# Which queue issues the stores of turned rows and of the softmax heads' outputs: GpSimd's in place of SP's

## The chip, the cores and the metric

The kernel runs on one core of one Trainium2 chip. The metric is the device time of one execution in microseconds, as the median of several runs. The engines are called PE (TensorE, with PEld for its weight loads), DVE (VectorE), ACT (ScalarE), POOL (GpSimd) and SP (SyncE). SP computes nothing here; it issues DMA transfers.

## The reference

One layer of a decoder: 512 tokens, width 2048, FFN width 5632, everything in float32.

```python
h = rms_norm(x, norm1_g)
qa, ka, va, ra, ga, qb, kb, vb = split(h @ w_in)
out_a = gla_mixer(qa, ka, va, ra, log_sigmoid(ga @ gla_gate_w2 + gla_gate_b) / 16)  # 4 heads, chunks of 64
out_b = dilated_mixer(rms_norm(qb), rms_norm(kb), vb, rel_bias)   # 8 softmax heads of width 128, three patterns
x = x + concat([out_a, out_b]) @ w_out
h2 = rms_norm(x, norm2_g)
x = x + (silu(h2 @ w_gate) * (h2 @ w_up)) @ w_down
```

## The kernel before

**Products.** All projections run as pairs of 512-column blocks. A pair is computed as seven block products P1 to P7 in the manner of Strassen (`Pair`, `stream`), so its operands are sums and differences of quarters of the rows, and its weights sums and differences of quarters of the weight matrix. Float32 is reached by splitting: every operand tile and every weight tile is parted into a high part (a cast on ACT, L174 for operands, L331 for weights, `wh`) and a low part (a subtraction on DVE, L175 and L335, `wl`). PE multiplies high by high and low, and low by high (L372). Weights come in quarters of 512 KB on SP's queue (L222, buffers `wa` to `wd`, 12 in all), and DVE forms their sums (L256). A product of PE on a `wl` can't start before DVE has made that `wl`, and DVE works in the order of its program.

**Stages.** In order of time:

- 0 to about 525 us: the input projection, five pairs and a first one of its own form; between its matmuls, the heads of the gated linear attention and the softmax heads (`dil_head`, two at a time, lanes 0 and 1). A softmax head's output `ot` (tile oT in lane 0, r in lane 1) is stored to `mix_d[4 + h // 2]` at L1040, 8 stores.
- to about 600: the last pair of the input projection, the gate (`final_gate`). The gated rows are transposed into tiles called `turned` and stored to `mix_d`, 8 stores. Meanwhile the operands of the output projection are read back from `mix_d` (`early_jobs` and `late_jobs`, loads at L1198 into `top` and r, at L1242 into work tiles v, T, qT, kT) and split.
- 600 to 745: two pairs of the output projection. `final_out` adds the residual; `first_columns` and `scaled_store` scale the rows, transpose them and store them to `xn_d`, 16 stores. They are read back as the operands of the FFN (`opn`). In the second pair `output_scales` computes the token scales `rs2`: two small additions on DVE (L1428, L1429) and five small operations on POOL (L158, L1431, L159, L1432, L1433).
- 745 to 1560: eleven FFN pairs of gate and up columns. `final_ffn` multiplies silu of the one by the other, transposes, and stores to `p_d`, 44 stores. `sums_job` reads `p_d` back a little later, forms the sums that the last projection needs, and stores them to `S_d`.
- 1560 to the end: the down projection, six pairs.

**Turned rows.** Everything that goes to `mix_d` from the gate, to `xn_d` and to `p_d` passes `transposed_store`: PE transposes 128x128 blocks (L1134), ACT evacuates them (L1142, or L1145 with gains) into oT and PT, of which there is one buffer each, or into a spare tile `turned`; then the tile is stored (L1149), as 256 rows of 1 KB. `done` records that these rows may be read back.

**Order.** `store` and `load` are both `nc.sync.dma_start` (L146, L147), so all stores and loads stand in one queue on SP, in the order of the program, and each waits at the head of that queue for what it needs. Side work (heads, operand jobs, sums) is kept in a list `background` and in lists of deferred steps (`later`, `soon`); `p.step()` lets some of it be written into the program in the middle of each weight tile's matmuls. A scheduler then orders the instructions within each engine.

POOL has little to do: two memsets, the reciprocal roots of the norms (`rsqrt_mean`, L157 to L159) and `output_scales`. It issues no store before the change.

Of the kernel before, what the change touches and what calls it, by code (L numbers as in the profile page):

```python
# [107 lines left out]
def block_kernel(ctx: ExitStack, tc: tile.TileContext, ins, out):  # L108
    nc = tc.nc
# [18 lines left out]
    def nm(s):  # L128
        uid[0] += 1
        return f"{s}_{uid[0]}"  # L130

    def dram(shape, name):
        return dr.tile(shape, F32, name=name, tag=name)

    def bank():
        return ps.tile([P, 512], F32, name=nm("bank"), tag="bank")

    def work(tag, shape=(P, 512), bufs=1):
        return mp.tile(list(shape), F32, name=nm(tag), tag=tag, bufs=bufs)
# [7 lines left out]
    store = nc.sync.dma_start  # L147
# [237 lines left out]
    def soon(fn, groups=1):  # L385

        soonest.append([groups, fn])
# [445 lines left out]
    mix_d = [dram([P, 2, 512], f"mix_d{b}") for b in range(8)]  # L833

    def head_cols(src, h, w=P):
        return src.rearrange("(t p) c -> p t c", p=P)[:, :, h * w : (h + 1) * w]
# [117 lines left out]
    def dil_head(h, lane):  # L954


        s = h // 4

        def tile_(name):
            if lane == 0:  # L960
                return work("oT" if name == "o" else name)
            if name in "qk":
                return work(name + "T")
            return rpool.tile([P, 512], F32, name=nm("r"), tag="r")

        def logits(b):
            if lane == 0:
                return work("L", bufs=2)
            return tile_("L") if b % 2 else work("PT")

        qh, kh, vh = tile_("q"), tile_("k"), tile_("v").rearrange("p (t d) -> p t d", t=4)
        load(qh.rearrange("p (t d) -> p t d", t=4), head_cols(proj[f"qb{s}"], h % 4))
        load(kh.rearrange("p (t d) -> p t d", t=4), head_cols(proj[f"kb{s}"], h % 4))
        load(vh, head_cols(proj[f"vb{s}"], h % 4))
        tb = tile_("T")
        load(tb, bass.AP(
            tensor=rep_d.tensor, offset=h * P * NB + P - 1, ap=[[NB - 1, P], [1, 512]]
        ))
        yield
        for src, g in ((qh, gq), (kh, gk)):  # L980
            tp = bank()
            for t in range(4):
                nc.tensor.transpose(tp[:, t * P : (t + 1) * P], src[:, t * P : (t + 1) * P], ident)
            nc.scalar.activation(src, tp, AF.Copy, scale=g)
        yield
        ot = tile_("o")
        lgs = {}

        def scores(b):
            n = P * (b + 1)  # L990
            lp = bank()
            nc.tensor.matmul(lp[:, :n], qh[:, b * P : (b + 1) * P], kh[:, :n], start=True, stop=True)  # L992
            lg = lgs[b] = logits(b)
            st = work("mx", (P, 4), bufs=4)

            def rest():
                nc.vector.tensor_tensor_reduce(
                    lg[:, :n], lp[:, :n], tb[:, 512 - n :], -1.0, 3.0e38, ALU.add, ALU.min,
                    st[:, 0:1],
                )  # L1000
                nc.scalar.activation(
                    lg[:, :n], lg[:, :n], AF.Exp, scale=-1.0, bias=st[:, 0:1],
                    accum_out=st[:, 2:3],
                )

                def scaled():
                    nc.vector.reciprocal(st[:, 3:4], st[:, 2:3])
                    nc.vector.tensor_scalar(lg[:, :n], lg[:, :n], st[:, 3:4], None, op0=ALU.mult)

                soon(scaled)  # L1010

            return rest

        def turn(b, tp):
            n = P * (b + 1)
            for k in range(b + 1):
                nc.tensor.transpose(  # L1017
                    tp[:, k * P : (k + 1) * P], lgs[b][:, k * P : (k + 1) * P], ident
                )
            return lambda: nc.scalar.copy(lgs[b][:, :n], tp[:, :n])  # L1020

        def values(b, op):
            for k in range(b + 1):
                nc.tensor.matmul(  # L1024
                    op, vh[:, k, :], lgs[b][:, k * P : (k + 1) * P], start=(k == 0), stop=(k == b)
                )
            return lambda: nc.scalar.copy(ot[:, b * P : (b + 1) * P], op)

        for i in range(6):
            rests = []  # L1030
            tp = bank() if 1 <= i <= 4 else None
            if i >= 2:
                op = tp[:, i * P : (i + 1) * P] if i < 4 else bank()[:, :P]
                rests.append(values(i - 2, op))
            if tp is not None:
                rests.append(turn(i - 1, tp))
            if i < 4:
                rests.append(scores(i))
            if i == 5:
                rests.append(lambda: store(mix_d[4 + h // 2][:, h % 2, :], ot))  # L1040
            yield rests

    def dil_heads(h):
# [83 lines left out]
    def transposed_store(tiles, half, dsts, gains=None, spare=None):  # L1127

        for b in range(2):
            bk = bank().rearrange("p (j n) -> p j n", j=2)  # L1130
            for jj in range(2):
                for m in range(2):
                    f = (2 * b + jj) * P
                    nc.tensor.transpose(  # L1134
                        bk[:, jj, m * P : (m + 1) * P], tiles[m][:, f : f + P], ident
                    )
            if spare is None:
                d = work(("oT", "PT")[b], (P, 2, 256))
            else:
                d = spare[:, b]  # L1140
            if gains is None:
                nc.scalar.copy(d, bk)  # L1142
            else:
                for jj in range(2):
                    nc.scalar.activation(  # L1145
                        d[:, jj, :], bk[:, jj, :], AF.Copy,
                        scale=gains[:, 2 * b + jj : 2 * b + jj + 1],
                    )
            store(dsts[b][:, :, half * 256 : (half + 1) * 256], d)  # L1149
            done.add((id(dsts[b]), half))  # L1150

    onorm = {}
# [7 lines left out]
    def final_gate(half, which, tiles, acc_):  # L1160
        og = onorm.pop((half, which))
        if tiles is None:
            tiles = [cpool.tile([P, 512], F32, name=nm("cr"), tag="C") for _ in range(2)]
            src = acc_
        else:
            src = tiles
        for m in range(2):
            if src is acc_:
                nc.vector.scalar_tensor_tensor(
                    halves(og[m]), unfolded(src[m]), row_scale(half, m), halves(og[m]),  # L1170
                    op0=ALU.mult, op1=ALU.mult,
                )
                neg = nrs1[:, 2 * half + m : 2 * half + m + 1]
                nc.scalar.activation(halves(tiles[m]), unfolded(src[m]), AF.Exp, scale=neg)
            else:
                nc.vector.tensor_tensor(og[m], src[m], og[m], op=ALU.mult)
                nc.scalar.activation(tiles[m], src[m], AF.Exp, scale=-1.0)
            nc.scalar.activation(tiles[m], tiles[m], AF.Ln, bias=1.0)
            nc.scalar.activation(tiles[m], tiles[m], AF.Exp, scale=-1.0)

        def rest():
            for m in range(2):
                nc.vector.tensor_tensor(tiles[m], tiles[m], og[m], op=ALU.mult)
            spare = apool.tile([P, 2, 2, 256], F32, name=nm("turned"), tag="A")
            later(1 + (src is tiles), lambda: transposed_store(
                tiles, half, mix_d[2 * which : 2 * which + 2], spare=spare
            ))

        soon(rest, 2)
# [153 lines left out]
    def scaled_store(tiles, rows, half, dsts, k0, tags=None):  # L1343
        xs = []
        for m in range(2):
            s = work(tags[m]) if tags else work("L", bufs=2)
            nc.scalar.activation(s, tiles[m], AF.Copy, scale=prox[:, rows[m] : rows[m] + 1])
            xs.append(s)
        return lambda: transposed_store(xs, half, dsts, g2[:, k0 : k0 + 4])
# [284 lines left out]
```

## Time and profile before

| | us |
|---|---|
| median of 3 runs | 1964.63 (1964.08 to 1965.51) |
| profiled execution, its own time | 1963.27 |
| span of the profiled execution | 1961.5 |

The mean granted clock of PE in it is 0.998. Views of the profile used below: the line of the engines gives busy time, its share of the span, and the number of instructions. Windows give, for a stretch of time, its length and the busy time of each engine, then the granted clock, the busy share of the DMA engines and GB/s. Waits give, for an engine and a line, what it waited for: the total, how many times, and the longest. The chain of waits lists what released what, ending with the last instruction. The timeline lists single instructions: start, length, engine, line, operation, output and inputs, and in brackets the idle time before it with what ended it. For a DMA that an engine issues, the timeline's length is the issue alone; the time until the data has landed stands in the chain and in the list of DMA issues.

### The profile page before, as it was taken

What the parts mean: (1) busy time and instruction counts of PE and PEld (TensorE: products, weight loads), DVE (VectorE), ACT (ScalarE), POOL (GpSimd) and SP (SyncE); (2) the same over time, 40 slices, a digit from 0 to 9 for tenths busy, and PEclk for the clock granted to TensorE, in tenths of its full rate; (3) what the DMA queues carried; (4) which work ended last, traced back from release to release, by engine and by line L of the source; (5) the groups of instructions that cost most, each with busy time, mean ns of one, the idle gap of its engine ahead of it and who ended that gap; (6) DMA issues with size and microseconds to landing.
All of it is one profiled execution on the core that took longest, in us unless ns stands there. A gap on an engine that the chain in (4) does not pass through costs nothing.

```text
span 1961.5 us, 25794 instructions
## 1 busy us (share of the span) xinstructions
PE 1924.8 (98%) x9226; PEld 1670.7 (85%) x9226; DVE 1653.7 (84%) x1851; ACT 1094.3 (56%) x1600; POOL 61.3 (3%) x81
## 2 busy tenths in 40 slices
PE   8999999999999999999999999999999999999999
PEld 6888888888878877888888888888888888888888
DVE  8997787868789889879878878878879989989987
ACT  8564564566766766545545445445546646546443
POOL 0000230010000000000000000000000000000000
PEclk9999999999999999999999999999999999999999
DMA  8457355464666685554553554554555865955761
GB/s 279 137 164 271 107 179 165 134 208 128 215 220 205 214 294 161 173 167 134 178 169 129 177 164 128 177 162 128 177 162 162 299 207 179 317 178 176 248 214 65
DMA packets 237258, 360.45 MB, mean 184 GB/s; under 512 B 18263, under 2 KB 97056, under 8 KB 237129
## 3 DMA queue, kind: packets, MB, share of 16 engines
q1 hardware_dynamic: 236776, 358.59, 57.2%
q8 instruction: 72, 1.18, 0.2%
q14 instruction: 58, 0.47, 0.1%
q10 hardware_dynamic: 352, 0.21, 0.0%
HBM read 296.59 MB, written 64.51 MB: 184 GB/s over the span
## 4 chain that ended last, share of the span: by engine, by line
PE 82%; DVE 8%; DMA 3%; issue 3%; ACT 2%; POOL 1%; SPq 0%; DVEq 0%; ACTq 0%
PE acc L372 74%; PE acc L440 3%; DVE wl L335 3%; DVE wa L256 2%; PE bank L1134 1%; DVE AS L175 1%; PE bank L992 1%; ACT wh L331 1%; DMA xn_d<-oT 1%; PE bank L1024 1%; DMA r<-xn_d 0%; PE bank L777 0%; PE bank L1017 0%; DMA qT<-S_d 0%; DVE AA L175 0%
## 5 line engine op out<-in xcount | busy, mean ns | idle before, releaser
L372 PE MATMUL acc<-wh,AS 128*128 128x512 f32 x3008 | 711.4, 379 | 0.7 <-ACT wh L331 0.6
L372 PEld LDWEIGHTS acc<-wh,AS 128*128 128x128 f32 x3008 | 569.0, 189 | 81.8 <-ACT wh L331 1.9
L331 ACT CAST wh<-wa 128x1024 fp32r<-128x1024 f32 x376 | 394.0, 1048 | 392.3 <-PE acc L372 366.6
L372 PE MATMUL acc<-wh,AA 128*128 128x512 f32 x2256 | 534.8, 380 | 0.0
L335 DVE TENSOR_TENSOR wl<-wa,wh 128x1024 fp32r<-128x1024 f32 x376 | 456.6, 1217 | 70.3 <-ACT wh L331 45.1
L372 PEld LDWEIGHTS acc<-wh,AA 128*128 128x128 f32 x2256 | 427.3, 190 | 61.1 <-ACT wh L331 0.6
L372 PE MATMUL acc<-wl,AS 128*128 128x512 f32 x1504 | 395.4, 385 | 10.4 <-DVE wl L335 10.1
L372 PEld LDWEIGHTS acc<-wl,AS 128*128 128x128 f32 x1504 | 279.5, 189 | 62.5 <-DVE wl L335 21.8
L372 PE MATMUL acc<-wl,AA 128*128 128x512 f32 x1128 | 297.3, 386 | 6.9 <-DVE wl L335 6.7
L372 PEld LDWEIGHTS acc<-wl,AA 128*128 128x128 f32 x1128 | 209.8, 189 | 39.1 <-DVE wl L335 10.1
L331 ACT CAST wh<-wb 128x1024 fp32r<-128x1024 f32 x94 | 98.5, 1049 | 130.1 <-PE acc L372 125.1
L331 ACT CAST wh<-wc 128x1024 fp32r<-128x1024 f32 x94 | 98.4, 1047 | 112.0 <-PE acc L372 104.9
L331 ACT CAST wh<-wd 128x1024 fp32r<-128x1024 f32 x94 | 98.5, 1048 | 105.5 <-PE acc L372 102.0
L256 DVE TENSOR_TENSOR wa<-wc,wa 128x1024 f32<-128x1024 f32 x94 | 114.5, 1222 | 46.0 <-DMA wc<-in_w_gate 24.8
L335 DVE TENSOR_TENSOR wl<-wc,wh 128x1024 fp32r<-128x1024 f32 x94 | 114.7, 1220 | 36.3 <-ACT wh L331 36.1
L335 DVE TENSOR_TENSOR wl<-wd,wh 128x1024 fp32r<-128x1024 f32 x94 | 114.4, 1220 | 35.7 <-ACT wh L331 28.9
L335 DVE TENSOR_TENSOR wl<-wb,wh 128x1024 fp32r<-128x1024 f32 x94 | 113.8, 1217 | 5.7 <-ACT wh L331 5.7
L256 DVE TENSOR_TENSOR wb<-wd,wb 128x1024 f32<-128x1024 f32 x94 | 114.4, 1217 | 1.0 <-DMA wd<-in_w_in 0.5
L256 DVE TENSOR_TENSOR wa<-wb,wa 128x1024 f32<-128x1024 f32 x94 | 113.6, 1219 | 0.8
L256 DVE TENSOR_TENSOR wa<-wd,wa 128x1024 f32<-128x1024 f32 x94 | 112.8, 1216 | 0.1
L298 DVE SCALAR_TENSOR_TENSOR seed<-acc,rs,seed 128x512 f32<-128x512 f32 x96 | 70.5, 745 | 24.6 <-PE acc L372 24.5
L282 ACT ACTIVATE seed<-acc,rs 128x512 f32<-128x512 f32 x96 | 60.6, 681 | 1.4 <-PE acc L372 0.8
(306 smaller groups left out, 1366.6 us busy)
## 6 DMA issues: line engine op xcount, KB each, us to landing
wa<-in_w_gate SPq DMA_DIRECT2D x44, 512.0 KB, 3.8
wb<-in_w_up SPq DMA_DIRECT2D x44, 512.0 KB, 4.1
wd<-in_w_up SPq DMA_DIRECT2D x44, 512.0 KB, 4.3
wc<-in_w_gate SPq DMA_DIRECT2D x44, 512.0 KB, 3.6
wc<-in_w_in SPq DMA_DIRECT2D x28, 512.0 KB, 3.7
wa<-in_w_in SPq DMA_DIRECT2D x24, 512.0 KB, 5.3
wb<-in_w_in SPq DMA_DIRECT2D x24, 512.0 KB, 6.0
wd<-in_w_in SPq DMA_DIRECT2D x24, 512.0 KB, 6.7
```

What stands on the lines that cost most here:

```text
L175: nc.vector.tensor_tensor(a[:, :, 1, :], src, a[:, :, 0, :].bitcast(F32), op=ALU.subtract)
L256: nc.vector.tensor_tensor(src, self.quarter(one, g), src, op=ALU.subtract)
L282: nc.scalar.activation(halves(t), unfolded(src[m]), AF.Copy, scale=self.scale(half, m))
L298: nc.vector.scalar_tensor_tensor(halves(seed[m]), unfolded(src[m]), self.scale(half, m), halves(seed[m]), op0=ALU.mult, op1=ALU.add,)
L331: nc.scalar.copy(high[k], sources[k])
L335: nc.vector.tensor_tensor(low[k], sources.pop(k), high[k].bitcast(F32), op=ALU.subtract)
L372: nc.tensor.matmul(p.dst[prod][m], a[:, jj, hl, m * P : (m + 1) * P], folded(w[:, jj, :]), start=fresh and g == 0 and len(terms) == 2 and ...
L440: recent["pe"] = nc.tensor.matmul(dst[prod][m], a[:, jj, hl, m * P : (m + 1) * P], folded(w[:, jj, :]), start=fresh and g == 0 and len(ter ...
L992: nc.tensor.matmul(lp[:, :n], qh[:, b * P : (b + 1) * P], kh[:, :n], start=True, stop=True)
L1024: nc.tensor.matmul(op, vh[:, k, :], lgs[b][:, k * P : (k + 1) * P], start=(k == 0), stop=(k == b))
L1134: nc.tensor.transpose(bk[:, jj, m * P : (m + 1) * P], tiles[m][:, f : f + P], ident)
```

## The change

Two stores go to `nc.gpsimd.dma_start` in place of `nc.sync.dma_start`. The store in `transposed_store` moves 68 stores (8 to `mix_d` from `turned`, 16 to `xn_d`, 44 to `p_d`), the one in `dil_head` 8 more. Each is 256 KB. Sizes, addresses and what is read back stay as they are, and all loads and all other stores stay on SP.

```diff
@@ dil_head
             if i == 5:
-                rests.append(lambda: store(mix_d[4 + h // 2][:, h % 2, :], ot))
+                rests.append(lambda: nc.gpsimd.dma_start(mix_d[4 + h // 2][:, h % 2, :], ot))
@@ transposed_store
-            store(dsts[b][:, :, half * 256 : (half + 1) * 256], d)
+            nc.gpsimd.dma_start(dsts[b][:, :, half * 256 : (half + 1) * 256], d)
             done.add((id(dsts[b]), half))
```

The scheduler answers with small changes of order: on DVE and ACT around 553 to 600 us and 735 to 750 us, on SP where the loads close up around the missing stores. In POOL's program two stores of `xn_d` from the second pair stand directly behind the five operations of `output_scales`.

## The prediction

> **What bounds the kernel now.** I read the engines' line first, then the windows, then the waits of PE and of SP's queue, then the chain of waits and, at the places it pointed to, the timeline.
>
> ```profile
> PE 1924.8 (98%) x9226; PEld 1670.7 (85%) x9226; DVE 1653.7 (84%) x1851; ACT 1094.3 (56%) x1600; POOL 61.3 (3%) x81
> ```
>
> PE is busy for 1924.8 of the span's 1961.5 us. All the time that a better placed store could give back is the difference, 36.7 us. A store that comes late costs only where PE then runs dry. The windows (length, then busy time of PE, PEld, DVE, ACT and POOL, the clock, the DMA share, GB/s) say where that is:
>
> ```profile
> 500.00:560.00 60.00, 58.05 (x331) 50.54 (x331) 42.35 (x77) 41.78 (x85) 0.00 (x0) 1.00 0.79 250
> 560.00:600.00 40.00, 34.00 (x146) 27.07 (x146) 39.06 (x47) 25.47 (x38) 0.00 (x0) 0.96 0.44 147
> 650.00:690.00 40.00, 37.34 (x185) 31.38 (x184) 34.34 (x37) 29.79 (x50) 2.96 (x2) 1.00 0.55 173
> 720.00:745.00 25.00, 19.10 (x92) 15.42 (x91) 18.07 (x25) 16.98 (x32) 2.30 (x3) 1.00 0.88 290
> 745.00:762.00 17.00, 15.86 (x72) 12.96 (x71) 17.00 (x20) 11.98 (x18) 2.26 (x3) 1.00 0.40 130
> 762.00:1480.00 718.00, 717.98 (x3399) 628.69 (x3400) 583.28 (x564) 359.78 (x407) 0.00 (x0) 1.00 0.52 159
> ```
>
> The reader is to see two regimes. From 762 to 1480 PE is never idle (717.98 of 718.00). Nothing can be gained there, and nothing lost earlier is won back there. Up to 762 PE has gaps: 1.95 and 6.00 us while the operands of the out projection are made (500 to 600), 2.66 around 670, 5.90 between 720 and 745, and 1.14 from there to 762, where DVE is busy for 17.00 of 17.00.
>
> **The part that is hidden.** 44 of the 76 moved stores are the FFN's (p_d, L1149). SP waits for ACT to fill them, and they land thus (count, size, median us from issue to landing):
>
> ```profile
> SPq L1149 <- ACT PT L1142: 103.2, 21, 10.4
> ```
>
> ```profile
> p_d<-oT SPq DMA_DIRECT2D x22, 256.0 KB, 2.4
> p_d<-PT SPq DMA_DIRECT2D x22, 256.0 KB, 3.0
> ```
>
> SP loses 103.2 us on these waits. In the changed order it goes past them, and then waits instead for the stores to land, because the loads of the same rows stand next for p_d. Weights may start earlier, but PE had them in time already. I cost these 44 stores at nothing. The cover is PE's full row of 718 us: a landing time doubled to 6 us still ends inside one pair's products. If that cover failed, the +0.5 worked out below would fall on each of the 11 pairs, 5.5 us.
>
> **The stores with a reader waiting.** What is left is 32 stores to mix_d and xn_d. Five of them stand in the chain of waits (start, us, what), each followed by the load that reads it back:
>
> ```profile
> 512.30 4.46 DMA mix_d<-r
> 516.84 4.50 DMA top<-mix_d
> ...
> 666.04 2.42 DMA xn_d<-oT
> 668.48 3.13 DMA r<-xn_d
> ...
> 717.51 5.20 DMA xn_d<-oT
> 722.73 3.53 DMA top<-xn_d
> ...
> 732.36 4.44 DMA xn_d<-oT
> ...
> 737.48 5.01 DMA r<-xn_d
> ```
>
> The time of PE that hangs on them is in PE's waits for the low weight part wl, from 510 to 600, from 640 to 700, and from 720 to 762 (us in total, times, longest):
>
> ```profile
> PE acc L372 <- DVE wl L335: 4.9, 6, 1.2
> ```
>
> ```profile
> PE acc L372 <- DVE wl L335: 1.0, 1, 1.0
> ```
>
> ```profile
> PE acc L372 <- DVE wl L335: 6.7, 4, 2.7
> ```
>
> DVE makes wl in its program's order, between the steps that read those loads. A late load therefore holds wl back, and wl holds PE.
>
> **The price of one store on GpSimd's queue.** The trace has no such store. The nearest rows are POOL's smallest pieces of work and SP's issue of the same store:
>
> ```profile
> 742.54 0.71 POOL L158 TENSOR_SCALAR rs<-tmp 128x4 f32<-128x4 f32 x1 [88.88 <-DVE tmp L1429]
> 743.34 1.05 POOL L1431 TENSOR_SCALAR part<-part 128x4 f32<-128x4 f32 x1
> 744.47 1.33 POOL L159 TENSOR_TENSOR rs<-rs,mhalf 128x4 f32<-128x4 f32 x1
> 745.78 1.23 POOL L1432 TENSOR_TENSOR part<-part,phalf 128x4 f32<-128x4 f32 x1
> 747.09 0.25 POOL L1433 TENSOR_TENSOR rs<-rs,part 128x4 f32<-128x4 f32 x1
> ```
>
> ```profile
> 744.62 0.56 SPq L1149 DMA_DIRECT2D xn_d<-oT  x1
> ...
> 747.09 0.57 SPq L1242 DMA_DIRECT2D v<-xn_d  x1
> ```
>
> If POOL needs 0.25 to 1.33 us to issue a store where SP needs 0.56, the store lands between 0.3 us earlier and 0.8 us later. I take +0.5 (the row of 1.05 less 0.56), because four of the five rows lie above SP's price. The Trainium skill, "DMA: Bandwidth & Descriptors", section "Specifications", gives a first byte at about 1 us on GpSimd's path and about 0.6 us on that of SP and ACT; by that the step would be +0.4, an estimate that no run here shows, and the sum below would fall by 5 × 0.1 = 0.5.
>
> **The five places.**
>
> At 512 ACT finished the output at 511.33, and SP, behind a weight load, stored it at 512.30:
>
> ```profile
> 511.06 0.27 ACT L1027 COPY r<-bank 128x128 f32<-128x128 f32 x1 [0.52 <-PE bank L1024]
> ```
>
> The store no longer waits for SP (−1.0) and pays +0.5. PE can win at most the stall behind it, and the six there have a mean of 4.9 / 6 = 0.8: I take −0.4, between 0 and −0.8.
>
> At 555 another softmax head's output is stored, read back as `top`, and split by ACT:
>
> ```profile
> 563.62 0.62 ACT L174 CAST AA<-top 128x512 fp32r<-128x512 f32 x1 [3.30 <-DMA top<-mix_d]
> 564.14 1.05 ACT L331 CAST wh<-wa 128x1024 fp32r<-128x1024 f32 x1
> ```
>
> The scheduler reorders ACT here: the cast of the next weights, wh, came right behind AA and now stands behind AA, three casts AS, two evacuations into `turned` and an Exp. Six further operations of about 0.6 us bound this at +3.7; the floor is 0, if wh isn't needed so soon. PE's longest stall there is 1.2 us and DVE is busy for 39.06 of 40.00 us, so most of the shift falls on a DVE that is late anyway. I take +1.0.
>
> At 666 the store has no queue to escape (it landed in 2.42) and ACT waits for its load: +0.5.
>
> At 717 and 732 the stores are slow, beside a DMA share of 0.88. At 717 the store pays +0.5, and a 512 KB weight load now stands ahead of `top` on SP, for another +0.2: +0.7. At 732 it pays +0.5, and two rows of DVE change places:
>
> ```profile
> 738.31 1.22 DVE L256 TENSOR_TENSOR wa<-wb,wa 128x1024 f32<-128x1024 f32 x1
> 741.69 0.69 DVE L1256 TENSOR_TENSOR r<-v,r 128x512 f32<-128x512 f32 x1 [2.16 <-DMA r<-xn_d]
> ```
>
> The weights' sum (1.22) now follows r's step, so the wait for r no longer covers it: +1.2. But two weight loads that stood around r's load are issued earlier, and r's 5.01 should fall to the 3.13 of the load at 668: −1.9. That makes −0.2, and +0.5 for both places.
>
> At 744 is the largest term. ACT had filled oT, SP issued the store at 744.62, and the loads v and qT followed at 747.09. On POOL the store stands in program order behind the five operations of output_scales quoted above, which end at 747.34. It doesn't depend on them; the engine works in order. It is held for 747.34 − 744.62 = 2.7 us and pays +0.5: +3.2. Queued behind it on POOL is only its neighbour (PT), which the second load, qT, waits for. These rows show why nothing absorbs it:
>
> ```profile
> 750.17 0.69 DVE L1260 TENSOR_TENSOR r<-v,r 128x512 f32<-128x512 f32 x1
> ```
>
> ```profile
> 753.79 1.13 PE L372 MATMUL acc<-wl,AS 128*128 128x512 f32 x4 [1.01 <-DVE wl L335]
> ```
>
> DVE takes v at 750.17, 3.1 us after its load was issued, which is what such a load takes (3.13); behind it stand a sum and a wl, and PE is already waiting for that wl. A late v is late PE.
>
> The sum: −0.4 + 1.0 + 0.5 + 0.5 + 3.2 = +4.8 us. The profiled execution took 1963.27 us around its span of 1961.5, and would take 1968.1. It lies 1.36 below the median of the runs, 1964.63, so on the median's scale the forecast is 1969.4.
>
> **The rivals.**
>
> *The landing is the gain (faster).* The stores at 512, 717 and 732 land in 4.46, 5.20 and 4.44 us against 2.42 at 666. If that is waiting in SP's ring behind 512 KB weight loads, a second ring passes them and their gaps close: the 6.7 us of 720 to 762 and 0.8 at 512 go, 7.5 in all, and 3.2 comes back at 744: −4.3, or 1960.3. For it: the fast landing is where the weight traffic is thin. Against it: at 720 to 745 the DMA share is 0.88, and a second ring shares the same engines. It decides once those landings fall below 3 us and the hold at 744 is no more than 3.2.
>
> *Both at once (no change).* If half of those gaps close, 3.3 us, and the hold at 744 stays as worked out, the sum is about +1.5, or 1966.1. For it: the two causes are independent, and the rows carry both.
>
> *POOL is slowed by DVE (slower still).* POOL's operations on 128x4 elements take 0.25 us or 1.33 while DVE is running operations of 1.22. If the making of a store's descriptors on POOL is held up by one such operation each time, each of the five places costs 1.2 more: +10.8, or 1975.4. The Trainium skill, "SBUF — State Buffer", section "SBUF: two separate sides", says that a DMA issued from GpSimd can't get its descriptors written while VectorE runs an operation that uses both ports. Its case is a copy; DVE's rows here are TENSOR_TENSOR, and no run shows it for them.
>
> **How the numbers follow.** My forecast has 0.40, the faster rival 0.16, no change 0.28, POOL slowed 0.16. The bound of what a measurement can tell is 0.2%, 3.9 us: below 1960.7 is faster, above 1968.6 slower. Faster 0.16, same 0.28, slower 0.40 + 0.16 = 0.56. Slower cases hold most of the chance, and the forecast's own range is 1967 to 1974: the unknown price of one store, −0.3 to +0.8, moves the five places by −4 to +1.5, of which I keep half at the lower end, and the bound at 555 adds 2.7. The whole range goes from the faster rival to a little above the slowest, 1960.0 to 1977.0; some 0.15 lies outside, half of the faster rival and part of the slowest.
>
> **What would show it.** In the profile after: the store at about 745 begins behind L1433 on POOL, v's load about 3 us later against the PE work around it, and PE's stall at 753.79 grows from 1.01 to about 4; PE's idle time from 762 to 1480 stays under 0.1; the landings of xn_d<-oT stay near 4 at 717 and 732. The forecast is wrong if those landings fall to 2.5 (faster, or no change), if the stores take far over 1 us on POOL (slower), or if gaps appear in the FFN's pairs, which I cost at nothing.

## The result, and the profile after

The kernel got slower by 11.3 us: 1975.96 us (median of 4 runs, 1974.25 to 1978.44) against 1964.70 (4 runs, 1964.08 to 1965.51). The ratio is 1.0056, 95% interval 1.0042 to 1.0070. The forecast was 1969.4: the direction was right, the size 4.7 to 4.8 us where 11.3 came.

The profiled execution after (the page's line of the engines, and from its list of DMA queues the one that is new):

```profile
span 1972.2 us, 25858 instructions
...
PE 1932.0 (98%) x9226; PEld 1670.9 (85%) x9226; DVE 1654.4 (84%) x1851; ACT 1094.7 (56%) x1600; POOL 113.3 (6%) x157
...
q0 software_dynamic: 6080, 19.93, 2.5%
```

POOL has 76 instructions more (157 against 81): the moved stores are there, in a queue of their own. The span grew by 10.7. The windows, at the same times as before:

```profile
500.00:560.00 60.00, 58.34 (x332) 50.60 (x331) 42.25 (x77) 41.84 (x85) 5.00 (x8) 1.00 0.78 249
560.00:600.00 40.00, 33.49 (x141) 26.54 (x139) 38.30 (x46) 24.48 (x37) 2.78 (x4) 0.91 0.45 148
650.00:690.00 40.00, 37.74 (x185) 31.57 (x184) 33.85 (x36) 31.04 (x53) 8.57 (x10) 1.00 0.50 166
720.00:745.00 25.00, 21.55 (x98) 17.79 (x96) 16.50 (x22) 15.06 (x28) 2.52 (x4) 0.93 0.84 293
745.00:762.00 17.00, 11.06 (x43) 9.13 (x44) 13.62 (x18) 9.63 (x16) 5.14 (x7) 0.90 0.48 162
762.00:1480.00 718.00, 716.39 (x3374) 623.20 (x3373) 582.35 (x562) 358.81 (x406) 25.43 (x36) 1.00 0.51 156
```

Two rows show the most. From 745 to 762 PE is busy for 11.06 us where it was 15.86, with 43 pieces of work done where it was 72. And the row of 718 us, full before (717.98), is no longer full: 716.39, with 3374 matmuls where there were 3399.

Set side by side, the same step of DVE comes later and later. It is level at 523 us, 1.1 us late at 573, 1.9 at 673, 3.2 when `top` is read (L215, at 726.36 before), 4.9 at r's second step (742.51), 6.8 at v's step (750.17), 9.1 at the third FFN pair's first sum (L1488, 975.49), 10.8 at the eighth's (1346.96), and 10.4 at the end. So some 7 us were lost ahead of 760 us and some 4 in the FFN, spread over its pairs. (Up to 1 us of the 7 need not come from the change: at 573 most kernels of the experiments below stand 1 us or more late, those that change nothing ahead of it too.)

PE's waits after, from 690 to 775 and from 775 to 1600 (us in total, times, longest; before, they were 6.7 and 0.3 us):

```profile
PE acc L372 <- DVE wl L335: 10.2, 4, 4.6
```

```profile
PE acc L372 <- DVE wl L335: 1.0, 3, 0.6
```

These waits don't make up the whole 10.7 us of the span. PE's idle time grew by 3.5 (from 36.7 to 40.2), and its busy time by 7.2 (from 1924.8 to 1932.0), for the same 9226 matmuls; the last section comes back to this.

**The place at 744.** The timeline of ACT, POOL, SP and DVE after:

```profile
746.07 0.83 ACT L1145 ACTIVATE oT<-bank,g 128x256 f32<-128x256 f32 x2
```

```profile
746.54 0.19 POOL L158 TENSOR_SCALAR rs<-tmp 128x4 f32<-128x4 f32 x1 [8.92 <-DVE tmp L1429]
746.82 0.19 POOL L1431 TENSOR_SCALAR part<-part 128x4 f32<-128x4 f32 x1
747.09 1.04 POOL L159 TENSOR_TENSOR rs<-rs,mhalf 128x4 f32<-128x4 f32 x1
748.11 1.96 POOL L1432 TENSOR_TENSOR part<-part,phalf 128x4 f32<-128x4 f32 x1
750.14 0.32 POOL L1433 TENSOR_TENSOR rs<-rs,part 128x4 f32<-128x4 f32 x1
750.72 0.73 POOL L1149 DMA_DIRECT2D xn_d<-oT  x1 [0.26 <-issue]
```

```profile
753.81 0.53 SPq L1242 DMA_DIRECT2D v<-xn_d  x1
```

```profile
756.93 0.69 DVE L1260 TENSOR_TENSOR r<-v,r 128x512 f32<-128x512 f32 x1 [2.45 <-DMA v<-xn_d]
```

The reader is to see the queue in program order. ACT has filled oT at 746.90, and the store starts at 750.72, 3.8 us later, right behind the last of output_scales' operations. Its load starts at 753.81, and DVE now idles 2.45 us for it, where before it had been just in time.

**The FFN.** One store of PT, its load and the first sum, before and then after:

```profile
893.57 0.59 ACT L1142 COPY PT<-bank 128x512 f32<-128x512 f32 x1
...
894.31 0.56 SPq L1149 DMA_DIRECT2D p_d<-PT  x1
896.97 2.54 SPq L1198 DMA_DIRECT2D r<-p_d  x4
...
901.19 0.69 DVE L1488 TENSOR_TENSOR r<-r,r 128x512 f32<-128x512 f32 x1
```

```profile
900.60 0.59 ACT L1142 COPY PT<-bank 128x512 f32<-128x512 f32 x1
...
901.10 0.69 POOL L1149 DMA_DIRECT2D p_d<-oT  x1 [9.82 <-ACT oT L1142]
901.70 0.81 POOL L1149 DMA_DIRECT2D p_d<-PT  x1
...
904.34 1.83 SPq L1198 DMA_DIRECT2D r<-p_d  x3
...
908.64 0.69 DVE L1488 TENSOR_TENSOR r<-r,r 128x512 f32<-128x512 f32 x1 [0.34 <-DMA r<-p_d]
```

What grew is the time from ACT's end to the store's start, 0.15 to 0.51. From the store's start to the load it is 2.66 us before and 2.64 after in this pair; in the other eight of the first nine pairs it was 2.45 before, so there another 0.2 comes from the landing. Before, DVE came to L1488 with no wait, but just in time: in the eight of these pairs whose landing the trace holds, the load that L1488 needs had landed 0.14 to 0.42 us earlier. Now DVE waits 0.34 us there. DVE's waits from 775 to 1600 show that this is so in nine pairs, and none is in the answer of before:

```profile
DVE r L1488 <- DMA r<-p_d: 2.5, 9, 0.4
DVE r L1490 <- DMA r<-p_d: 1.1, 1, 1.1
```

### The profile page after: what moved, and what is told of

Its sections match the earlier page's. It is cut to its first block, busy times and chain, and to the rows that moved or that the text cites. A ratio compares the mean times of both kernels' runs of the same rounds, so it can differ in the third digit from the quotient of the medians.

```text
span 1972.2 us, 25858 instructions
## 1 busy us (share of the span) xinstructions
PE 1932.0 (98%) x9226; PEld 1670.9 (85%) x9226; DVE 1654.4 (84%) x1851; ACT 1094.7 (56%) x1600; POOL 113.3 (6%) x157
## 4 chain that ended last, share of the span: by engine, by line
PE 49%; issue 35%; DVE 4%; POOL 2%; DMA 2%; ACT 1%; SPq 0%; DVEq 0%; POOLq 0%; ACTq 0%
PE acc L372 45%; DVE wl L335 2%; POOL p_d L1149 1%; DVE wa L256 1%; PE bank L992 1%; DMA mix_d<-r 1%; PE bank L1024 1%; POOL xn_d L1149 0%; DVE AS L175 0%; DMA q<-in_x 0%; PE bank L1017 0%; DMA top<-mix_d 0%; PE bank L1134 0%; PE bank L910 0%; PE bank L983 0%
## 5 line engine op out<-in xcount | busy, mean ns | idle before, releaser
L372 PE MATMUL acc<-wl,AS 128*128 128x512 f32 x1504 | 396.5, 386 | 10.4 <-DVE wl L335 9.7
```

Source lines behind the costliest of these rows:

```text
L372: nc.tensor.matmul(p.dst[prod][m], a[:, jj, hl, m * P : (m + 1) * P], folded(w[:, jj, :]), start=fresh and g == 0 and len(terms) == 2 and ...
```

## The experiments

All ratios are to the kernel before on the same chip, with 95% intervals; the us beside them are the ratio's excess times 1964.7. Executions scatter by some 2 us around their median, so that differences under about 2 us between two kernels are not told apart by their times. The traces tell more, and are used for that.

**One group of stores at a time.** The common edit gives `transposed_store` an argument:

```diff
-    def transposed_store(tiles, half, dsts, gains=None, spare=None):
+    def transposed_store(tiles, half, dsts, gains=None, spare=None, put=store):
...
-            store(dsts[b][:, :, half * 256 : (half + 1) * 256], d)
+            put(dsts[b][:, :, half * 256 : (half + 1) * 256], d)
```

The 44 FFN stores, with `put=nc.gpsimd.dma_start` in `final_ffn` alone:

> Only the 44 FFN stores (p_d) are issued on GpSimd's queue. The lag theory (a store on GpSimd's queue starts 0.35 us later after ACT than on SP's, and the first step of the sums on DVE, L1488, has no slack for it): each of the eleven pairs grows by 0.3 to 0.4 us, so 3.5 to 4.5 us in all, about 1968.7. The theory of the prediction (these stores are hidden): 0 to 0.5 us, about 1965. A theory by which the lost time sits only ahead of 762 us gives the same 1965.

Measured: 1.0014 (1.0005 to 1.0023), +2.8 us. In its trace DVE waits for the loads at L1488 in 7 pairs, 1.8 us in all, and its lateness against the kernel before grows from 2.5 us at 742 to 5.5 at 1422. The stores that the prediction took as hidden are not.

The 16 stores to xn_d, with the same `put` in `scaled_store` alone:

> Only the 16 stores to xn_d move. The lag theory alone, 0.4 us at each of five links: +2 us, 1966.7. Lag together with POOL's program order (the store held behind output_scales) and the later output_scales: +5 to +6 us, 1970. If the time in the full change came from the two kinds of mix_d stores, 1965.

Measured: 1.0035 (1.0022 to 1.0047), +6.9 us, the largest part.

The 8 softmax heads' stores, with the change's first hunk alone:

> Only the 8 stores of the softmax heads' outputs move. Lag theory: the store at 512 us gains up to 1 us by not waiting for SP and the one at 555 loses 0.4; the sum lies within 0.5 us of no change, 1964.2 to 1965.2. If the reordered ACT cast at 564 us (taken at +1.0) comes from this store alone: 1965.7.

Measured: 1.0007 (0.9998 to 1.0016), +1.4 us. The interval holds no change; that the store at 512 would gain isn't seen.

The 8 stores of the gated rows, with `put` in `final_gate` alone:

> Only the 8 stores of the gated rows to mix_d move. Lag theory: their readers come microseconds later, so 0 to 0.4 us, 1964.7 to 1965.1. If the reordered ACT cast at 564 us belongs to them: 1965.7. A theory by which every store on GpSimd's queue slows the engines around it gives 8/76 of 11.3 us, +1.2, 1965.9.

Measured: 1.0005 (0.9997 to 1.0014), +1.0 us. This interval, too, holds no change.

The four add up to 12.1 us, against 11.0 by the ratio of the full change. No interaction between the groups is seen, but with intervals of 2 us to either side one of a few us could hide.

**Time from ACT's end to the load that reads the store back.** The traces of the two kernels and of ten experiments, some of them below, all have the places of the prediction. From the end of ACT's evacuation to the start of the first load of these rows, in us (lowest and highest, number of traces; for the FFN the usual value of the first nine pairs):

```
place                     stored on SP          stored on GpSimd's queue
666                       2.44 to 2.47  (7)     2.74 to 2.87  (5)
717                       5.24 to 5.86  (7)     6.00 to 6.44  (5)
732                       3.15 to 4.48  (7)     5.03 to 6.02  (5)
744                       2.50 to 4.11  (8)     5.41, 5.97, 6.91; 3.29 ahead of output_scales
FFN, PT to r              2.6                   3.16
```

Apart from the 3.29, where nothing holds the store, the two columns don't overlap in any row. At 666, with little else under way, the store pays 0.3 to 0.4 us, all of it between ACT's end and the store's start. In the FFN PT's store stands behind oT's on POOL, and it is 0.56. At 717 and 732, beside the weight loads, it is 0.8 and 1.1 us (medians): there the landing, too, is slower than in SP's ring, not faster (from the store's start 5.6 to 6.0 against 5.2 to 5.8 at 717, 4.6 to 5.6 against 3.1 to 4.5 at 732). DVE pays for it: between 673 and 742, DVE falls back by another 1.8 to 2.9 us against the kernel before in the five traces that have these stores on GpSimd's queue, and gains 0.2 to 1.4 on it in the seven that have them on SP's (the run with the later FFN stores, below, is one of them).

Something else changes at 732. Before, one weight load stood ahead of the store on SP (728.46) and one behind it (734.26). In the full change SP issues two ahead of it, and POOL's store comes after both:

```profile
731.17 1.40 SPq L222 DMA_DIRECT2D wd<-in_w_up  x2
```

```profile
735.68 0.69 POOL L1149 DMA_DIRECT2D xn_d<-oT  x1 [14.53 <-ACT oT L1145]
```

How much of the slower landing is the other queue and how much the weight loads that moved ahead is not shown.

**The hold behind output_scales.** In this kernel the 16 xn_d stores are on GpSimd's queue and output_scales is called after the store:

```diff
                 def rest():
                     turn()
+                    if which == 0 and half == 1:
+                        output_scales()
...
                 later(2, rest)
-                if which == 0 and half == 1:
-                    output_scales()
```

> The 16 stores to xn_d on GpSimd's queue, and output_scales called after the second pair's store in place of before it, so that its five operations on POOL stand behind the two stores and not ahead of them. If the hold by POOL's program order makes the last part of the loss (the store issued about 3.9 us after ACT had filled oT): 2 to 3.5 us less than with the 16 stores alone, so 1.002 of the kernel before, about 1968. If the lag of each store and the later chains ahead of it make the loss: no change against the 16 stores alone, 1.0035.

Measured: 1.0028 (1.0017 to 1.0039), +5.5 us, 1.4 less than the 16 stores alone, which the times don't tell from nothing. The trace does tell: POOL, then SP, then ACT.

```profile
746.43 0.69 POOL L1149 DMA_DIRECT2D xn_d<-oT  x1 [9.56 <-ACT PT L1145]
```

```profile
749.32 0.53 SPq L1242 DMA_DIRECT2D v<-xn_d  x1
```

```profile
754.45 1.27 ACT L282 ACTIVATE seed<-acc,rs 128x512 f32<-128x512 f32 x2 [4.00 <-POOL rs L1433]
```

The store is no longer held (ACT ended at 746.03), and v's load comes 3.29 us after ACT's end. But rs2 is late now, and ACT idles 4.00 us for it. So the hold goes with POOL's program order, and this order only hands the delay to the next reader.

Then the two stores behind output_scales by themselves, and the other 14 by themselves (`put` chosen in `final_out` by `which == 0 and half == 1`):

> Only the two stores to xn_d that stand behind output_scales in POOL's program are issued there; everything else on SP. If the hold by POOL's program order is worth what the trace suggests (v's load starts 6 to 7 us after ACT has filled oT, against 2.5 to 4.1 with the store on SP): 2 to 4 us slower, 1.001 to 1.002. If the loss of the 16 stores comes from the slower landings at 717 and 732 us: no change.

Measured: 1.0009 (1.0000 to 1.0018), +1.8 us.

> The complement: 14 stores to xn_d on GpSimd's queue, the two behind output_scales on SP. If hold and landings are separate causes and add, this one and the two stores alone make up the 6.9 us of the 16: 3 to 5 us slower, 1.0015 to 1.0025. If the hold is all: no change. If rival one of the prediction held here, a second ring that passes the weight loads: faster.

Measured: 1.0010 (1.0001 to 1.0019), +2.0 us. Neither interval reaches below no change, though the first begins at it, so hold and late landings are most likely two causes, the hold the less certain: in the traces DVE loses 1.5 to 3.0 us between r's second step and v's where the store is held (three traces), and −0.6 to 1.6 where it stands on SP (eight). The sum of the two runs, 3.8, lies below the 6.9 of the 16 together; the intervals (0 to 3.5, 0.2 to 3.7, 4.3 to 9.2) don't exclude that they simply add, and whether the two are worth more together stays open.

**Slack in the FFN.** One more step in `sums_job`, with the FFN's stores on GpSimd's queue and, as a control, on SP:

```diff
             done.add((id(sums_d[j][name]), 0))

         yield
         yield
+        yield
```

> The 44 FFN stores on GpSimd's queue, and one more step between the loads of sums_job and its first sum on DVE, so that L1488 and its fellows stand one weight tile later in DVE's order. Lag theory: the 0.35 us per pair find slack; the growth per pair is gone and the kernel stands at the time of the same step added with the stores on SP, within 0.5 us. If GpSimd's queue costs something else per pair (contention on DVE, ACT or the DMA engines): 2 to 4 us above that, as without the step.

> The control: all stores on SP as before, and the same one more step in sums_job. Lag theory: before, L1488 came just in time and PE never waited in the FFN, so the step changes nothing, 0.9995 to 1.0005. If the FFN of the kernel before had a hidden loss there: up to 2 us faster.

Measured: 1.0001 (0.9992 to 1.0010) and 0.9995 (0.9986 to 1.0004), 0.2 us slower and 1.0 us faster than the kernel before, both not told from no change. In the first the loads come as late as ever (3.16 us behind ACT), but DVE meets them one weight tile later, without a wait (L1489 is this kernel's line of the first sum):

```profile
903.57 0.69 DVE L1489 TENSOR_TENSOR r<-r,r 128x512 f32<-128x512 f32 x1
```

The traces say the same more sharply. From 760 to 1500 us, past nine of the eleven pairs, DVE's lateness against the kernel before grows by 4.6 us in the full change and by 2.8 with the FFN's stores alone; in the nine traces with the FFN's stores on SP or with the third step it changes by 0.3 or less. So the FFN's loss is missing slack at one step of DVE; these runs show nothing else that the queue does there.

**A later store still.** To lengthen the lag, POOL copies a part of PT ahead of PT's store:

```diff
+            if b == 1 and put is not store:
+                nc.gpsimd.tensor_copy(lagt, d[:, 0, :112])
             put(dsts[b][:, :, half * 256 : (half + 1) * 256], d)
```

> The 44 FFN stores on GpSimd's queue, and a copy of 128x112 elements of PT on POOL ahead of each store of PT, so that 22 of the stores start 0.7 to 1.1 us later still. If the sums of the FFN have no slack (what a store loses, the pair loses): each of the eleven pairs grows by another 0.7 to 1.1 us, 8 to 12 us above the 44 stores alone, some 1976 to 1980. If the 0.35 us per pair had another cause (queue or port contention): within 2 us of the 44 stores alone.

Measured: 1.0521 (1.0507 to 1.0535), +102 us, or 9.3 per pair. The expected copy of under 1 us is there in half of the cases; in the other half it takes 6.8 (POOL, then DVE):

```profile
894.57 0.66 POOL L1150 COPY lagt<-PT 128x112 f32<-128x112 f32 x1
...
905.80 6.78 POOL L1150 COPY lagt<-PT 128x112 f32<-128x112 f32 x1
```

```profile
910.08 2.36 DVE L256 TENSOR_TENSOR wa<-wd,wa 128x1024 f32<-128x1024 f32 x2
919.28 0.69 DVE L1491 TENSOR_TENSOR r<-r,r 128x512 f32<-128x512 f32 x1 [6.84 <-DMA r<-p_d]
```

The size was missed, for a reason told at the end. What the run was for still shows: the load comes 9.7 us behind ACT where it came 3.16, DVE idles 6.8 us for it, and the pair loses more than that. It is the same chain, from POOL's store to L1491 (this kernel's line of the first sum) to wl to PE. What makes the other 2.5 us per pair was not looked into; PE's granted clock in this run has a mean of 0.975.

**Another queue.** The same 76 stores on `nc.scalar.dma_start`:

> The same 76 stores issued on ACT's queue, by the engine that fills the tiles. If the loss belongs to GpSimd's queue (its lag, and POOL's program order): gone, 1964 to 1966. If it belongs to leaving SP's queue at all (the scheduler's new order, weight loads ahead of the loads that read back): 5 to 7 us remain, 1970. ACT also pays an issue for each store; at 0.5 us each on an engine that is 56% busy this should be hidden except beside the casts near 720 to 760, 1 us at most.

Measured: 1.0026 (1.0015 to 1.0037), +5.1 us. Neither side has it all. In the FFN ACT's queue has no lag (2.6 us, as on SP). But at 732, where the weight loads are under way, the store on ACT's queue and its load on SP are 8 us apart:

```profile
733.94 0.52 ACTq L1149 DMA_DIRECT2D xn_d<-oT  x1
```

```profile
741.90 0.52 SPq L1198 DMA_DIRECT2D r<-xn_d  x1
```

It is 3.15 to 4.48 when SP issues both, and the chain of waits gives the landing of this store as 7.94 us. So a part of the loss is not GpSimd's: here, too, a store outside SP's queue landed later while weights were loaded. The scheduler's order changes with it (two weight loads stand ahead of these loads on SP), and the two were not taken apart.

**The full change, mended at two places.** The two stores behind output_scales stay on SP, and sums_job has its third step:

> The full change with its two dearest places mended: the two stores behind output_scales stay on SP, and sums_job has one more step between its loads and its first sum. If hold and missing slack make the better part of the 11 us: what is left is the 14 other stores to xn_d, the heads' and the gate's stores, 2.0 + 1.4 + 1.0 = 4.4 us by their own runs, 1.001 to 1.004. If the loss is spread over all stores on GpSimd's queue, as a lag that adds whatever the readers do: 9 us or more, 1.0045 to 1.006. Faster than the kernel before by neither.

Measured: 1.0017 (1.0008 to 1.0026), +3.3 us of the 11. The two places make the better part: 7.7 us are recovered, more than the 1.8 and 2.8 that the two cost by their own runs, which again leaves open whether the hold costs more beside the other late stores than alone. No kernel that was run is faster than the kernel before by more than its interval, so there is no version to prefer to it.

## Why the prediction was right in sign and short in size

Its steps, each with what came.

- **44 FFN stores at nothing.** This is the step that failed: +2.8 us by their own run, about 4 in the profile of the full change. The prediction took PE's full row (717.98 of 718.00) for a cover. It is none: a row that is just full says that PE is fed in time, not how long ahead. The slack is at the reader, L1488 on DVE, which came without a wait, but with 0.14 to 0.42 us of reserve, against loads that now come 0.56 later; DVE was busy through the whole stretch ahead of it, and wl stood behind it. The prediction named what would be lost if the cover failed, 0.5 on each of the 11 pairs or 5.5 us, and gaps in the FFN's pairs as a sign of being wrong; it should have looked for the first reader of the loads.
- **The price of a store on GpSimd's queue, +0.5.** Right in size, 0.3 to 0.4 at 666 and 0.56 in the FFN, but partly by luck. The prediction looked for it in the length of the issue, which is mostly 0.69 us on POOL against 0.56 on SP; most of it lies between ACT's end and the start of that issue. The Trainium skill ("DMA: Bandwidth & Descriptors", "Specifications") gives a first byte at about 1 us on GpSimd's path and about 0.6 on SP's, a difference of 0.4 by estimate. The size agrees, but in these traces it lies ahead of the store's start and hardly in its landing, which is 2.4 to 2.7 us on both queues where little else loads.
- **717 and 732, +0.5 together.** Mis-sized: DVE fell from 1.9 to 4.9 us late across them, 3.0. The price beside weight loads is not 0.5 but 0.8 and 1.1, and the −1.9 for r's load did not come: r's second step came 5.8 us after its load was issued (741.58 to 747.37). The weight loads did move ahead, as forecast, but ahead of the store as well.
- **744, +3.2.** The mechanism was right: the store stood behind output_scales. It was held for 3.8 us, not 2.7: ACT's end came 2.3 us later than before, the end of output_scales 3.1 (750.46 against 747.34), and the store began 0.26 behind that. On DVE the place added 1.9 us, and the two stores alone cost 1.8 (0 to 3.5). It was thus over-sized; a likely reason is that v's step was late already by what 717 and 732 had done.
- **512, −0.4; 555, +1.0; 666, +0.5.** DVE was level at 523, 1.1 late at 573, and 1.3 to 1.9 across 666. No gain at 512: the store began 0.4 us earlier (511.89 for 512.30), but its read-back 1.6 later (518.41 for 516.84). At 555 wh was late as forecast, and PE waited 1.67 us for it; but PE's longest stall there before was 1.8 us, for the transposes, and not the 1.2 for wl that the prediction read. The sizes of 555 and 666 fit, but such steps within one trace are as large in kernels that change nothing there (the one with the FFN's stores alone is 2.5 us late at 742), and no run proves them.
- **Rivals.** A second ring that passes the weight loads: refuted, at 717 and 732 every store on GpSimd's queue was later than every one on SP's. POOL slowed by DVE gave 1975.4, near the result, but by another way: each store's issue took 0.54 to 0.90 us, also in the middle of DVE's work. Nor were POOL's own operations slower as a whole: L1432 took 1.96 where it had taken 1.23, L158 and L1431 took 0.19 each where they had taken 0.71 and 1.05, and the five together took 3.9 where they had taken 4.8. That the time came near this rival's is luck. PE's stall at v's wl was forecast to grow from 1.01 to about 4; it grew to 1.69, and it was the one before it, behind r, that grew more, from 2.71 to 4.61.

## What to carry to other kernels

A full row of the bounding engine is no slack: before a transfer is called hidden, find the first instruction that reads it, and how long that instruction would otherwise have waited. Work on an in-order queue waits for whatever stands ahead of it in program order, so list that for each place, not for one. Don't count on a store landing sooner off a queue that also loads: here it landed no sooner, and later beside heavy loads.

## What the runs showed of the hardware

A POOL copy of 128x112 elements that reads SBUF took 0.66 us or 6.8 (two of the 22 took 7.8 and 13.8). The long one above ended at 912.58, when DVE's unbroken row of TENSOR_TENSOR had ended at 912.44, and all 22 copies, short and long, ended 0.14 us behind such an end: a copy was held through what was left of the row. What ended the row in the long cases was DVE's wait at L1491, for the load of the very rows whose store stood behind the copy, so the copy went on only when DVE had run out of work. The Trainium skill, "SBUF — State Buffer", says that tensor_tensor with both inputs in SBUF contends with GpSimd's reads, and that the later one blocks until the first finishes; here it blocked not for one instruction but until DVE paused. The issue of a store on POOL in the same stretch (0.69 us at 905.24) wasn't held.

PE's granted clock fell with the stalls: 0.93 and 0.90 from 720 to 745 and from 745 to 762, where it had been 1.00. It can fall with shorter ones: in the kernel before it was 0.84 from 565 to 575, where PE's longest wait was 1.8 us. Behind the longest stall the four matmuls of one product took 2.08 us where they had taken 1.13:

```profile
749.25 2.08 PE L372 MATMUL acc<-wl,AA 128*128 128x512 f32 x4 [4.61 <-DVE wl L335]
```

PE's busy time grew by 7.2 us with the same 9226 matmuls, so a part of the loss stands in the profile as work and not as waiting. Matched matmul by matmul, 2.6 of it lie between 720 and 762 and 3.1 between 762 and 1480, where the windows give the clock as 1.00; what lengthens them there is not shown.
